# Moving the activation slots of a fused conv-attention block to one residue modulo 512

## The chip, the cores and the metric

The kernel runs on one core of one Trainium2 chip. The metric is the device time of one execution in microseconds; the kernel before took 2053.18 us (median of 3 runs, 2053.03 to 2053.26). The engines are named as in the profile: PE is TensorE (matmuls), PEld its weight loads, DVE is VectorE, ACT ScalarE, POOL GpSimd, SP the queue that issues the transfers.

## What is computed

One decoder block on x of 2,048 positions by 1,024 channels, float32. Two branches share one input projection of 7,680 columns and are merged by gates:

```
h    = rmsnorm(x) ; proj = h @ w_in            # 1024 x 7680
glu_in, conv_gate, q, k, v, attn_gate, merge = split(proj)
c    = silu(layernorm(depthwise_conv31(a * sigmoid(b))))
y_c  = (c * silu(conv_gate)) @ w_conv_out
att  = sliding-window attention (window 128, 16 heads, 4 kv heads, sinks)
y_a  = (att * silu(attn_gate)) @ w_attn_out
x    = x + (g_conv * y_c + g_attn * y_a) @ w_out ; out = rmsnorm(x)
```

## The kernel before

**Order of the work.** The sequence is taken in two sweeps of 1,024 positions. A sweep holds its normalised input transposed in 16 tiles `hT[half][k]`: half 0 or 1 for its 512 positions, k for the chunk of 128 input channels. It runs the 60 projections of 128 output columns, then 8 `ya` projections on the attention output `aT`, 8 `yc` projections on the gated convolution output `uT`, and last the output product `o`: 16 blocks of 24 matmuls, 384 in a sweep. The order on PE is written out by hand: the class `Line` keeps an estimated clock (`MM_US = 0.2275` for a matmul) and puts the steps of the attention, of the convolution and of the norms between the matmuls at due times. Attention is 32 units in a sweep, each with three visits to PE: scores `sc` (16 matmuls of 256 columns or fewer), transposes `tpp` (4 of 128 columns), and `ov` (4 matmuls of 512 columns, weights `vt` twice and `vd` twice).

**One projection.** Every product is made of three matmuls, since each operand is split into a high and a low part (`float32r`). In `project` (line 281) a half is 8 chunks by 3 matmuls, 24, each with its own weight load, all into one PSUM tile:

```
for half in halves:
    for k in range(KC):
        ... (whi, r[:, 0, :]), (whi, r[:, 1, :]), (wlo, r[:, 0, :])
            pe.matmul(out=ps, lhsT=a, rhs=b, ...)
```

The moving operand `r` is 512 columns of 4 bytes, 2,048 bytes of a partition: the high part begins at the start of a slot, the low part 2,048 bytes behind. The weights (`whi`, `wlo`) are 128 columns, 512 bytes, of a buffer of the pool `stage`, which starts where the slots end; chunk k lies at 512 times (k modulo 4) in it. In `o` (line 885) the moving operand is `wo` in a `c` slot and the weights are a 512-byte piece of `mT` in an `a` or `h` slot. In `ov` (line 622) the moving operands are `pt` and `pc`, the weights `vt` and `vd`, all in slots.

**Slots.** The pool `slots` has 43 buffers, named h0 to h15, a0 to a15, c0 to c7 and x0 to x2, each used by several tiles in turn. Normally a slot is 4,096 bytes of every partition. The 12 names in `WIDE` (all c, a14, a15, h14, h15) are 4,224 bytes, for a tile of 1,054 elements: the convolution's input `glu` with a halo of 30. `glu` only ever lies in c6, c7 and a14. The buffers lie behind one another in the order in which the program first asks for them; the first starts at byte 9,024 of the partition, which is 320 modulo 512 (and 832 modulo 2,048). Each wide slot pushes everything behind it by 128 bytes modulo 512. The starts modulo 512, in order:

| slots | before | after |
|---|---|---|
| a0-a5, h0-h7, a11, a12, a7-a10, c0 | 320 | 320 |
| c1 | 448 | 320 |
| c2 | 64 | 320 |
| c3 | 192 | 320 |
| c7 | 320 | 320 |
| h8-h14 | 448 | 320 |
| h15 | 64 | 320 |
| a6, a13, x0, x1, x2, a15 | 192 | 320 |
| c6 | 320 | 320 |
| a14 | 448 | 320 |
| c4 | 64 | 320 |
| c5 | 192 | 320 |
| raw, whi, wlo buffers | 320 | 320 |

**Which tile lies where.** In sweep 0 `hT` and later `uT` have half 0 in h0-h7 and half 1 in h8-h15; in sweep 1 half 0 in h8-h15 and half 1 in a0-a7. `aT` (and `mT`) lie in a0-a15 in sweep 0 and in h0-h7, a8-a15 in sweep 1. `vt` lies in a0-a3 (sweep 1: h0-h3), `vd` in x0-x2 and a15, `pt` and `pc` in a7-a10 (sweep 1: h7, a8-a10). Each `wo` chunk k lies in c0 to c7.

Of the kernel before, what the change touches and what calls it, by code (L numbers as in the profile page):

```python
# [19 lines left out]
P = 128  # L20
# [3 lines left out]
T = 1024  # L24
# [4 lines left out]
HALO = TAPS - 1  # L29
# [24 lines left out]
def hybrid_block(ctx: ExitStack, tc: tile.TileContext, x, par_d, w_in, w_conv, sinks, w_attn, w_out,  # L54
# [21 lines left out]
    A = [f"a{i}" for i in range(16)]  # L76
    C = [f"c{i}" for i in range(8)]
    X = [f"x{i}" for i in range(3)]
    WIDE = set(C) | {"a14", "a15", "h14", "h15"}

    def slot(tag, shape, dt, name):
        n = int(np.prod(shape[1:]))
        full = HALO + T + 2 if tag in WIDE else 1024
        t = slots.tile([P, full], dt, tag=tag, name=name)
        v = t[:, 0:n]
        if len(shape) == 3:
            v = v.rearrange("p (a b) -> p a b", b=shape[2])
        elif len(shape) == 4:
            v = v.rearrange("p (a b c) -> p a b c", b=shape[2], c=shape[3])
        return v  # L90
# [11 lines left out]
    def load_first(half):  # L102
        xs = []
        for j in range(4):
            r0 = (4 * half + j) * P
            xs.append(slot(A[7 * half + j], [P, D], F32, f"xf{half}_{j}"))
            nc.sync.dma_start(out=xs[-1], in_=x2[r0:r0 + P, :])
        return xs
# [4 lines left out]
    ident_r = const.tile([P, P], F32R, name="ident_r")  # L113
    ident = f(ident_r)
    ident_0 = slot(A[4], [P, P], F32, "ident_0")
    make_identity(nc, ident_0)
    dve.tensor_copy(out=ident_r, in_=ident_0)
    ones_0 = slot(A[5], [P, P], F32, "ones_0")
    dve.memset(ones_0, 1.0 / D)
    ones = const.tile([P, P], F32R, name="ones")  # L120
# [844 lines left out]
```

## Time and profile before

| | |
|---|---|
| median of 3 runs | 2053.18 us |
| the profiled execution's own time | 2053.2 us |
| its span, first to last instruction | 2051.5 us |
| granted TensorE clock, mean | 0.999 |
| matmuls | 9,256 |
| bytes moved | 355.91 MB, 173 GB/s mean |

The profiled execution stands 0.02 us from the median, and 1.7 us of its time lie around its span. Busy time of PE is modelled at the end of each matmul, so what is read below is the distance from the start of one matmul to the start of the next: the number of matmuls that begin in a stretch, against the length of the stretch. In a table of stretches the number in brackets behind x counts every matmul that is in work in the stretch, also one that began ahead of it.

### The profile page before, as it was taken

How to read it: one execution, taken by the hardware profiler on the slowest of the kernel's cores; microseconds unless marked ns; L12 is line 12 of the kernel's file. 1: busy time of each engine (PE TensorE's matmuls, PEld its weight loads, DVE VectorE, ACT ScalarE, POOL GpSimd, SP SyncE). 2: the span in 40 equal slices, each digit the busy share in tenths (PEclk: the TensorE clock that was granted, in tenths of full speed). 3: DMA queues.
4: the chain of work that ended last, by engine and by line, in shares of the span. 5: the costliest groups of instructions: out<-in, count | busy, mean ns of one | idle time of the engine just before them, and what ended most of it. 6: DMA issues, size and time to landing. Idle time of an engine off the chain costs nothing.

```text
span 2051.5 us, 27562 instructions
## 1 busy us (share of the span) xinstructions
PE 2031.3 (99%) x9256; PEld 1669.1 (81%) x9256; DVE 1327.4 (65%) x1965; ACT 1027.8 (50%) x2313; POOL 403.4 (20%) x336
## 2 busy tenths in 40 slices
PE   7999999999999999999999999999999999999998
PEld 6888888888888888888888888888888888888886
DVE  4968769988994355123668678689888924441323
ACT  6312477777777463123433125767677764621222
POOL 2335332333323223241001120111011100001200
PEclk9999999999999999999999999999999999999999
DMA  7445655555566757444344555555555577564422
GB/s 249 144 144 167 208 170 160 166 168 172 161 188 212 252 174 244 143 157 169 131 144 138 164 178 188 160 175 174 173 156 171 179 222 257 172 228 138 153 110 82
DMA packets 265821, 355.91 MB, mean 173 GB/s; under 512 B 28112, under 2 KB 126544, under 8 KB 265680
## 3 DMA queue, kind: packets, MB, share of 16 engines
q1 hardware_dynamic: 265680, 354.16, 53.3%
q8 instruction: 73, 1.20, 0.2%
q14 instruction: 68, 0.56, 0.1%
HBM read 234.51 MB, written 119.54 MB: 173 GB/s over the span
## 4 chain that ended last, share of the span: by engine, by line
PE 96%; DVE 2%; DMA 1%; issue 0%; SPq 0%; POOL 0%; ACT 0%; DVEq 0%; POOLq 0%
PE mm_cg L281 9%; PE o L885 9%; PE mm_ma L281 9%; PE mm_ga L281 9%; PE mm_mc L281 9%; PE mm_yc L281 9%; PE mm_ya L281 9%; PE mm_gb L281 8%; PE mm_ag L281 7%; PE mm_q_a L281 4%; PE mm_q_b L281 4%; PE sc L572 3%; PE ov L622 3%; PE mm_v L281 2%; DVE acc L396 2%; PE tpp L602 1%
## 5 line engine op out<-in xcount | busy, mean ns | idle before, releaser
L396 DVE SCALAR_TENSOR_TENSOR acc<-glu,par,acc 128x1024 f32<-128x1024 f32 x464 | 596.3, 1285 | 6.2
L885 PE MATMUL o<-wo,mT 128*128 128x512 f32 x768 | 181.3, 395 | 0.0
L885 PEld LDWEIGHTS o<-wo,mT 128*128 128x128 f32 x768 | 143.2, 188 | 32.0
L281 PE MATMUL mm_cg<-hT,whi_cg 128*128 128x512 f32 x512 | 161.1, 396 | 0.0
L281 PE MATMUL mm_ga<-hT,whi_ga 128*128 128x512 f32 x512 | 160.9, 395 | 0.2 <-ACT whi_ga L253 0.2
L281 PE MATMUL mm_ma<-hT,whi_ma 128*128 128x512 f32 x512 | 161.0, 396 | 0.0
L281 PE MATMUL mm_ag<-hT,whi_ag 128*128 128x512 f32 x512 | 160.8, 395 | 0.0
L281 PE MATMUL mm_gb<-hT,whi_gb 128*128 128x512 f32 x512 | 160.7, 395 | 0.0
L281 PE MATMUL mm_mc<-hT,whi_mc 128*128 128x512 f32 x512 | 159.7, 393 | 0.0
L281 PE MATMUL mm_yc<-uT,whi_yc 128*128 128x512 f32 x512 | 159.5, 393 | 0.0
L281 PE MATMUL mm_ya<-aT,whi_ya 128*128 128x512 f32 x512 | 158.7, 391 | 0.0
L613 POOL TENSOR_SCALAR_AFFINE_SELECT pc<-pt 128x1024 fp32r<-128x1024 f32 x60 | 65.6, 1094 | 428.7 <-DVE pt L242 428.6
L281 PEld LDWEIGHTS mm_yc<-uT,whi_yc 128*128 128x128 f32 x512 | 96.2, 188 | 21.8
L281 PEld LDWEIGHTS mm_mc<-hT,whi_mc 128*128 128x128 f32 x512 | 96.1, 188 | 21.7
L281 PEld LDWEIGHTS mm_ya<-aT,whi_ya 128*128 128x128 f32 x512 | 96.1, 188 | 20.9
L281 PEld LDWEIGHTS mm_ga<-hT,whi_ga 128*128 128x128 f32 x512 | 94.6, 188 | 20.4 <-ACT whi_ga L253 0.6
L281 PEld LDWEIGHTS mm_gb<-hT,whi_gb 128*128 128x128 f32 x512 | 94.7, 188 | 19.9
L281 PEld LDWEIGHTS mm_ag<-hT,whi_ag 128*128 128x128 f32 x512 | 94.3, 188 | 19.4
L281 PEld LDWEIGHTS mm_cg<-hT,whi_cg 128*128 128x128 f32 x512 | 94.2, 188 | 19.5
L281 PEld LDWEIGHTS mm_ma<-hT,whi_ma 128*128 128x128 f32 x512 | 94.2, 188 | 19.3
L592 ACT ACTIVATE ss<-ss,st 128x128 f32<-128x128 f32 x256 | 99.7, 391 | 11.2 <-DVE st L587 10.7
L281 PE MATMUL mm_ga<-hT,wlo_ga 128*128 128x512 f32 x256 | 100.8, 394 | 0.7 <-POOL wlo_ga L242 0.7
(364 smaller groups left out, 4259.3 us busy)
## 6 DMA issues: line engine op xcount, KB each, us to landing
qk<-d_q SPq DMA_DIRECT2D x256, 64.0 KB, 2.2
d_a<-ss SPq DMA_DIRECT2D x128, 128.0 KB, 1.9
aT<-d_a SPq DMA_DIRECT2D x32, 512.0 KB, 5.5
qk<-d_k SPq DMA_DIRECT2D x240, 64.0 KB, 2.0
raw_gb<-in_w_in_dram SPq DMA_DIRECT2D x34, 256.0 KB, 3.2
raw_ga<-in_w_in_dram SPq DMA_DIRECT2D x34, 256.0 KB, 3.3
raw_ag<-in_w_in_dram SPq DMA_DIRECT2D x32, 256.0 KB, 3.7
d_ag<-ag SPq DMA_DIRECT2D x32, 256.0 KB, 2.2
```

The source lines that it names most:

```text
L281: pe.matmul(out=ps, lhsT=a, rhs=b, start=(k == 0 and i == 0), stop=(k == KC - 1 and i == 2))
L396: dve.scalar_tensor_tensor(out=to, in0=glu[c][:, j:j + T], scalar=tap(c, j), in1=acc[c], op0=ALU.mult, op1=ALU.add)
L572: pe.matmul(out=o, lhsT=q[:, h, :], rhs=r, start=(j == 0), stop=(j == 1))
L592: act.activation(out=sb[:, h, :], in_=sb[:, h, :], func=AF.Exp, scale=SCALE, bias=ngm[:, h:h + 1], accum_out=den[:, h:h + 1])
L602: pe.transpose(out=tpp[:, h, :], in_=sb[:, h, :], identity=ident)
L613: pool.affine_select(out=pc, in_=f(pt), pattern=[[0, 2], [0, GQ], [1, P]], compare_op=ALU.is_ge, fill=0.0, base=0, channel_multiplier=-1)
L622: pe.matmul(out=ov, lhsT=vv, rhs=pp[:, i % 2], start=(i == 0), stop=(i == nm - 1))
L885: pe.matmul(out=ps, lhsT=a[:, c0:c0 + P], rhs=r, start=(k == 0 and i == 0), stop=(k == KC - 1 and i == 2))
```

## The change

The set of wide slots shrinks from twelve to the three that hold a `glu` tile, and those three grow from 4,224 to 4,608 bytes, which is 512 more than the others have. Three times 512 bytes are twelve times 128 bytes, so the pools behind the slots stay where they are. No instruction, wait, transfer or order changes; only the addresses of 22 slots do (the right column of the table above).

```
-    WIDE = set(C) | {"a14", "a15", "h14", "h15"}
+    WIDE = {"c6", "c7", "a14"}

     def slot(tag, shape, dt, name):
         n = int(np.prod(shape[1:]))
-        full = HALO + T + 2 if tag in WIDE else 1024
+        full = 1024 + P if tag in WIDE else 1024
```

## The prediction

> **What bounds the kernel now.** I read the page's busy shares and its clock line first, then the chain that ended last, then what PE waited for.
>
> ```profile
> span 2051.5 us, 27562 instructions
> PE 2031.3 (99%) x9256; PEld 1669.1 (81%) x9256; DVE 1327.4 (65%) x1965; ACT 1027.8 (50%) x2313; POOL 403.4 (20%) x336
> PEclk9999999999999999999999999999999999999999
> PE 96%; DVE 2%; DMA 1%; issue 0%; SPq 0%; POOL 0%; ACT 0%; DVEq 0%; POOLq 0%
> ```
> ```profile
> PE tpf L361 <- DVE ident_r L117: 8.4, 1, 8.4
> PE tpf L361 <- DVE xf L354: 2.4, 2, 1.5
> PE sc L572 <- DVE pt L242: 1.0, 1, 1.0
> PE mm_ga L281 <- POOL wlo_ga L242: 0.7, 1, 0.7
> PE tpf L361 <- DVE hT L364: 0.5, 1, 0.5
> PE mm_ga L281 <- ACT whi_ga L253: 0.2, 1, 0.2
> ```
>
> PE is the chain (96%). Its waits come to 13.2 us, 11.3 of them transposes of the opening (tpf); behind that it waits 1.9 us in two milliseconds. The clock is full in every slice. So the time is the number of matmuls times the distance between their starts, and the change can only act through that distance, or by making another engine late. The pieces of the chain give the distance:
>
> ```profile
> 147.28 11.04 PE mm_q_b L281 x48
> ...
> 764.63 87.99 PE mm_ya L281 x384
> 852.62 88.33 PE mm_yc L281 x384
> ...
> 1160.36 11.07 PE mm_q_b L281 x48
> ...
> 1779.53 87.67 PE mm_ya L281 x384
> 1867.19 88.57 PE mm_yc L281 x384
> 1955.77 88.72 PE o L885 x384
> ```
>
> These stretches hold matmuls of 512 columns with nothing between, at one clock, and yet run at 228.3 ns (87.67/384), 230.0, 230.7 and 231.0 ns. So I cut them into halves of 24 matmuls. In the table of stretches (length, PE busy, x in work, clock, transfers) one of the x is the matmul of the half before whose modelled end reaches in:
>
> ```profile
> 880.00:885.59 5.59, 5.59 (x25) 1.00 0.26 91
> 885.59:891.04 5.45, 5.45 (x25) 1.00 0.58 196
> 1900.24:1905.82 5.58, 5.58 (x25) 1.00 0.72 238
> 1905.82:1911.31 5.49, 5.49 (x25) 1.00 0.12 40
> 1375.84:1376.75 0.91, 0.91 (x5) 1.00 0.03 9
> 1376.75:1377.69 0.94, 0.94 (x5) 1.00 0.00 0
> 422.34:423.73 1.39, 1.39 (x8) 1.00 0.50 189
> 425.08:426.45 1.36, 1.36 (x7) 1.00 0.71 185
> 593.07:598.51 5.44, 5.44 (x25) 1.00 0.53 149
> ```
>
> Rows 1 and 2 are yc in sweep 0: half 1, with uT in h8-h15 (448, last chunk 64), takes 5.59 us, and half 0 in h0-h7 (320, as the weights) 5.45. Rows 3 and 4 are yc in sweep 1, where the places are swapped: now half 0 lies in h8-h15 and takes 5.58, half 1 in a0-a7, with only a6 off 320, 5.49. So it isn't the half, the sweep or the weights, which are the same, but the place of the moving tile. The two halves make the rows of 48 above: 5.59 + 5.45 is 11.04 and 5.58 + 5.49 is 11.07. Transfers don't explain it: the row with the busiest DMA (0.72) and the one with 0.26 are equally slow.
>
> Rows 5 and 6 turn the pair round: in one attention unit the four matmuls ahead of `ov` (moving and weights on 320) take 0.91, then `ov` itself 0.94, whose moving tiles lie on 320 while its last two weights, `vd`, lie on 192. So it is the pair of moving tile and weights that matters, not the moving tile alone. Rows 7 and 8 show six matmuls right behind a score visit, and six further on in the same half, all on 320: 1.39 and 1.36. A visit costs 0.03 until the rhythm is found again. Row 9 is a half on 320 within the attention stage: 5.44, 226.7 ns, the best there is.
>
> **The change part by part.** It adds and removes no instruction, wait or transfer; no queue is passed. What moves is the start of 22 slots, and every matmul of 512 columns gets the residue of row 2 for both operands. Gains, from the rows above, a half being 24 matmuls:
>
> 1. Sweep 0, half 1 (h8-h15): 60 projections and 8 yc, 68 halves × (5.59 − 5.45) = 9.5 us.
> 2. Sweep 1, half 0 (h8-h15): 68 × (5.58 − 5.45) = 8.8.
> 3. Sweep 1, half 1 (a6 off): 68 × (5.49 − 5.45) = 2.7.
> 4. ya: 384 matmuls at 5.45/24 = 227.1 ns would be 87.2 against 87.99 and 87.67: 1.3.
> 5. o: 88.72 − 87.2 = 1.5 in sweep 1, taken twice: 3.0. This is the least certain, see the rivals.
> 6. ov: 60 units with vd × 0.03 = 1.8, and the rhythm that needn't be found again behind it, another 0.03 each by rows 7 and 8: 1.8.
>
> Together 28.9. Off go the places where the rhythm is lost anyway: 64 score visits, 64 tpp and 32 other groups of transposes, 160 × 6 = 960 matmuls. Half of them lie in halves now off 320, and there six take 6 × 232.9 = 1.40, no more than the 1.39 with all on 320; the gain of 5.8 ns each, counted above, isn't there: 480 × 5.8 = 2.8 off. Half of term 5 goes off for its doubt, 1.5. That leaves 24.6; I take 24.
>
> The other engines. DVE, ACT and POOL instructions read and write slots that move. No row shows one of them by its slot, so this is bounded by size: the dearest is
>
> ```profile
> L396 DVE SCALAR_TENSOR_TENSOR acc<-glu,par,acc 128x1024 f32<-128x1024 f32 x464 | 596.3, 1285 | 6.2
> ...
> 226.00:420.00 194.00, 193.03 (x915) 160.00 (x915) 172.40 (x249) 138.53 (x337) 56.17 (x49) 1.00 0.54 172
> 420.00:560.00 140.00, 140.00 (x667) 115.97 (x666) 125.41 (x189) 100.06 (x247) 43.52 (x36) 1.00 0.53 168
> 1240.00:1480.00 240.00, 240.00 (x1139) 198.94 (x1138) 206.48 (x313) 168.90 (x415) 24.99 (x21) 1.00 0.56 172
> ```
>
> with 31 taps that start at 31 different offsets of 4 bytes and one mean of 1285 ns. One per cent more or less on its 596 us is 6 us on an engine that idles for 700: nothing, as long as DVE stays behind PE. Its fullest stage is 125.41 of 140 (90%); with PE 1.2% quicker that is 91%. So DVE, ACT and transfers are costed at nothing; the cover is this 9%, some 13 us of a stage of 140, and if it were gone PE's 1.0 us wait of sc on pt is the one that would grow. Behind the gain nothing else is late next: PE stays the chain. The transfers keep count, sizes and queue; each projection's weights are asked for one projection (11 us) ahead.
>
> One rule speaks against all of this. The Trainium skill, page "TensorE: Matmul & The Clock Gate", section "Step-by-step: what each phase is for", says that PE has two independent SBUF read ports, so that loading the next weights takes no read bandwidth from the running matmul. By it alone addresses shouldn't matter and the sum would be 0; rows 1 to 6 don't agree, unless something else than the address sets them apart.
>
> **The rivals.** *A, only the residue modulo more than 512 counts.* All moving tiles that are quick now start at 832 modulo 2,048. After the change h8-h15, a6, a13, x, a15 and c6 start at 1,344, a14 at 1,856, c4 and c5 at 320. If the moving tile needs 832, terms 1 to 4 fall away and only ov (3.6) and part of o stay: 2049. For it:
>
> ```profile
> 1959.76:1961.85 2.09, 2.09 (x10) 1.00 1.01 320
> ```
>
> nine matmuls of o in sweep 1 on c6, c7 and c0, all 320 modulo 512 with weights on 320, but 1,856, 1,344 and 832 modulo 2,048: 231.9 ns each, no rhythm found. Against it: within every half the weights step through all four multiples of 512 (chunk k at 512 times k modulo 4), and rows 2 and 9 stay at 5.45 and 5.44, so at least the weights' residue above 512 is free. And the nine of o come behind matmuls on slots off 320, so at least six of them are still finding the rhythm, as in row 7.
>
> *B, nothing happens.* Moving reads and weight loads don't touch each other, and something else than the residue slows h8-h15 (their place high in the partition, say, as all quick moving tiles lie low): 2053. The rule cited above would leave the time there. Against it ov, where weights low and high in the partition make the difference while the moving tile stays.
>
> *C, slower.* The new distance between h8-h15 and the weights locks into a worse rhythm than now, as the pair in ov does: 0.94/4 = 235.0 ns against 232.9 on terms 1 and 2, 136 halves × 24 × 2.1 ns = 6.9, so 2060. It decides from the point where a half on h8-h15 takes over 5.59. Only the ov row speaks for it, and that pair ends with this change.
>
> **How the numbers follow.** The profiled execution took 2053.2, 0.02 over the median: 2053.2 − 24 = 2029. Chances: forecast 0.83, A 0.07, B 0.06, C 0.04. Its own range: the low end is every half at 5.44 and no rhythm lost, 28.9 + 304 halves × 0.01 = 31.9, so 2021; the high end is that only the halves away from the attention gain, some 32 projections a sweep (18 ahead of it, 6 behind, 8 yc) × (0.14 + 0.13 + 0.04) = 9.9, and ya 1.3, so 2042. A lies beyond at 2049 and isn't needed for 8 in 10, so the range is 2021 to 2042. A measurement of this kernel can tell 0.2%, 4.1 us, from no change: faster is the forecast and a third of A, 0.85; same is B and the rest of A, 0.11; slower is C, 0.04.
>
> **What would show it.** Right: the chain's rows of 48 fall from 11.04 and 11.07 to 10.88 to 10.90 in both sweeps, yc and ya to 87.1 or 87.2, o to 87.2 to 88; halves 0 and 1 are alike; ov's four take 0.91; DVE's and ACT's means stay. Wrong: halves on h8-h15 stay at 5.58 (A or B; then ov tells them apart, 0.91 in A and 0.94 in B) or rise (C), or new waits of PE on DVE or ACT appear. Only o staying at 88.7 would mean that term 5 alone was wrong.

## The result, and the profile after

The changed kernel takes 2027.62 us (median of 4 runs, 2027.36 to 2027.86) against 2053.18: 25.56 us less, a ratio of 0.9876 with a 95% interval of 0.9858 to 0.9893. The forecast was 2029, range 2021 to 2042.

The page after, and PE's waits. The span is 25.6 us shorter, PE is still 99% busy, the clock is full, and the waits are the old ones: 13.8 us in place of 13.2.

```profile
span 2025.9 us, 27562 instructions
PE 2004.9 (99%) x9256; PEld 1666.9 (82%) x9256; DVE 1324.1 (65%) x1965; ACT 1026.0 (51%) x2313; POOL 403.4 (20%) x336
PEclk9999999999999999999999999999999999999999
...
L396 DVE SCALAR_TENSOR_TENSOR acc<-glu,par,acc 128x1024 f32<-128x1024 f32 x464 | 595.9, 1284 | 6.2
```
```profile
PE tpf L361 <- DVE ident_r L117: 8.4, 1, 8.4
PE tpf L361 <- DVE xf L354: 2.3, 2, 1.4
PE sc L572 <- DVE pt L242: 1.3, 1, 1.3
PE tpf L361 <- DVE hT L364: 0.9, 1, 0.9
```

The chain's pieces after. Every undisturbed row of 48 is 10.88 and every row of 384 is 87.04 or 87.05, 226.67 ns from start to start, in both sweeps and in all three products, which ran at 228.3 to 231.0 ns before. This steady distance is what is called the rhythm here and in the prediction:

```profile
145.72 10.88 PE mm_q_b L281 x48
...
756.66 87.04 PE mm_ya L281 x384
843.70 87.04 PE mm_yc L281 x384
...
1147.03 10.88 PE mm_q_b L281 x48
...
1757.77 87.04 PE mm_ya L281 x384
1844.81 87.04 PE mm_yc L281 x384
1931.85 87.05 PE o L885 x384
```

Halves of yc as in the prediction (half 0 and 1 in sweep 0, half 0 and 1 in sweep 1), then the ov of its row 6. All halves take 5.44, ov 0.91:

```profile
876.18:881.62 5.44, 5.44 (x25) 1.00 0.62 199
881.62:887.06 5.44, 5.44 (x25) 1.00 0.22 79
1877.29:1882.72 5.44, 5.44 (x25) 1.00 0.69 241
1882.72:1888.16 5.44, 5.44 (x25) 1.00 0.14 49
1360.45:1361.36 0.91, 0.91 (x5) 1.00 0.00 0
```

Transfers at a share of 0.14 and of 0.69 leave a half at 5.44 alike.

Where the 25.6 us came from, by the sum of the distances between starts of matmuls in the two traces (first to last matmul: 2035.71 us before, 2010.12 after):

```
                                   before   after    less   term of the prediction
projections, yc  sweep 0 half 1    381.29   372.75   8.53   1:  9.5
                 sweep 1 half 0    381.03   372.85   8.18   2:  8.8
                 sweep 1 half 1    375.63   372.59   3.04   3:  2.7
                 sweep 0 half 0    376.27   375.24   1.03   none
ya                                 175.65   174.08   1.57   4:  1.3
o                                  178.44   175.54   2.90   5:  3.0, half taken off
ov                                  57.80    56.21   1.59   6:  3.6 with what follows it
score visits                        61.58    62.81  -1.22   none
transposes, layernorm                                -0.03
sum                                                 25.6    24.6, taken as 24
```

### The profile page after: what moved, and what is told of

It is laid out like the page before. It is cut to its first block, busy times and chain, and to the rows that moved or that the text cites. A ratio compares the mean times of both kernels' runs of the same rounds, so it can differ in the third digit from the quotient of the medians.

```text
span 2025.9 us, 27562 instructions
## 1 busy us (share of the span) xinstructions
PE 2004.9 (99%) x9256; PEld 1666.9 (82%) x9256; DVE 1324.1 (65%) x1965; ACT 1026.0 (51%) x2313; POOL 403.4 (20%) x336
## 4 chain that ended last, share of the span: by engine, by line
PE 94%; DVE 4%; DMA 1%; issue 0%; ACT 0%; SPq 0%; POOL 0%; DVEq 0%; ACTq 0%; POOLq 0%
PE mm_ma L281 9%; PE o L885 9%; PE mm_mc L281 9%; PE mm_yc L281 9%; PE mm_ya L281 9%; PE mm_ga L281 9%; PE mm_gb L281 8%; PE mm_cg L281 8%; PE mm_ag L281 6%; PE mm_q_a L281 4%; PE mm_q_b L281 4%; PE sc L572 3%; DVE acc L396 3%; PE ov L622 2%; PE mm_v L281 2%; PE tpp L602 1%
## 5 line engine op out<-in xcount | busy, mean ns | idle before, releaser
L396 DVE SCALAR_TENSOR_TENSOR acc<-glu,par,acc 128x1024 f32<-128x1024 f32 x464 | 595.9, 1284 | 6.2
L281 PEld LDWEIGHTS mm_ag<-hT,whi_ag 128*128 128x128 f32 x512 | 94.2, 188 | 18.3
```

Of the source, the lines that this page charges most:

```text
L281: pe.matmul(out=ps, lhsT=a, rhs=b, start=(k == 0 and i == 0), stop=(k == KC - 1 and i == 2))
L396: dve.scalar_tensor_tensor(out=to, in0=glu[c][:, j:j + T], scalar=tap(c, j), in1=acc[c], op0=ALU.mult, op1=ALU.add)
```

## The experiments

Left open by the result: whether the start of the moving tile or its distance from the weights counts, modulo what, which of the weight loads it is that counts, and whether another distance is better still. Names: theory P is the distance, R the start itself. In all of these kernels instructions and order are those of the changed kernel; unused buffers are laid between the others to move them.

**Everything moved by 128 bytes.**

```
     dve.memset(v_last, 0.0)
+    const.tile([P, 32], F32, name="pad")
```

> The changed kernel with 128 bytes more ahead of the slots, so that every slot and every weight buffer starts at 448 modulo 512, the residue on which h8-h15 were slow before. Theory P (the distance between the moving tile and the weights modulo 512 counts; it is still 0): 2027.6 us, at most 1 us off, halves of 24 matmuls at 5.44 us. Theory R (the start of the moving tile itself counts, and 320 is a good one, 448 a bad one): every half at 5.58 to 5.59, 304 halves x 0.145 = 44 us more, and o 768 x 6 ns = 5 us more, about 2076 us.

2027.93 us, ratio to the kernel before 0.9878 (0.9862 to 0.9895); two halves of yc in sweep 0:

```profile
875.40:880.85 5.44, 5.44 (x25) 1.00 0.62 201
880.85:886.28 5.44, 5.44 (x25) 1.00 0.25 74
```

On 448, the residue that h8-h15 had when they were slow, everything is as quick as on 320. R falls.

**Only the weights moved by 128 bytes.**

```
+    stage.tile([P, 32], F32, tag="pad", name="pad", bufs=1)
     x2, out2 = x[0], out[0]
```

> The changed kernel with 128 bytes more between the slots and the weight buffers: all slots stay at 320, raw, whi and wlo go to 448. Theory P: all 304 halves of the projections, ya and yc go from 5.44 to about 5.58, 44 us more, about 2071 us, slower than the kernel before, while o (weights and moving tile both in slots) stays at 87.05 us for 384 matmuls and ov's four matmuls at 0.91 us. Theory R: no change, 2027.6 us.

2064.79 us, slower than before the change: 1.0057 (1.0042 to 1.0072). Halves 0 and 1 of yc in sweep 0, and the chain's pieces of sweep 1:

```profile
892.38:897.95 5.57, 5.57 (x25) 1.00 0.60 192
897.95:903.53 5.58, 5.58 (x25) 1.00 0.25 82
```
```profile
1790.46 89.23 PE mm_ya L282 x384
1879.69 89.22 PE mm_yc L282 x384
1968.91 87.05 PE o L886 x384
```

No moving tile was touched and all projections are slow; o, whose two operands lie in slots, is not. That is P. The size was missed by 6 us. Away from the attention the matmuls of the projections lose 5.9 ns each, as the 44 us have it; the 3,483 between the first and the last attention unit of a sweep lose 4.5, which makes 5.4 us less. Near the attention's visits the rhythm is lost anyway, as in the main result.

**Only h8-h15 put back to 448.** Pads of 128 bytes ahead of h8 and 384 behind h15.

> The changed kernel with only h8 to h15 put back to 448 modulo 512, all else at 320. If terms 1 and 2 of the prediction are sized right (136 halves on h8-h15, 0.13 to 0.14 us each, 18.3 us), and the halves behind them lose their first few matmuls again (0.01 to 0.03 each), then 2046 to 2050 us; yc 11.03 to 11.04 us per projection in both sweeps. Were h8-h15 not the place of the gain, it would stay below 2035 us. Theories P and R say the same here.

2047.59 us, 0.9973 (0.9963 to 0.9984). yc, halves 0 and 1 of sweep 0, then of sweep 1:

```profile
884.93:890.38 5.46, 5.46 (x25) 1.00 0.58 194
890.38:895.97 5.59, 5.59 (x25) 1.00 0.27 79
1896.41:1902.00 5.59, 5.59 (x25) 1.00 0.77 235
1902.00:1907.45 5.46, 5.46 (x25) 1.00 0.16 41
```

The slow halves go with h8-h15 from half 1 to half 0. The eight slots are worth 20.0 of the 25.6 us. The well-placed halves take 5.46 instead of 5.44: their first three matmuls, behind a slow half, take 231, 232 and 230 ns from start to start, the others 227.

**Other distances, three and three and two in one kernel.** Pads of other sizes at the same places; for 16 bytes the view of h0-h7 starts 4 elements into the slot.

> Three distances in one kernel: h0-h7 start 64 bytes above the weights' residue, h8-h15 192, a0-a15 and c0-c3 256. Read from the quiet yc: sweep 0 half 0 is 64, half 1 192; sweep 1 half 0 192, half 1 256. Theory P with a period of 512: all three slow, 5.50 to 5.62 us for 24 matmuls, the whole 2055 to 2080 us. Theory P with a shorter period: 256 (period 256) or 64, 192 and 256 (period 64) as quick as 5.44.

> As the last one with 96 on h0-h7, 448 on h8-h15 and 32 on a0-a15. Theory P with a period of 512 and a sharp optimum at 0: all slow, 5.50 to 5.62. If what counts is the same 64-byte piece, 32 is as quick as 5.44 and 96 and 448 are slow. A distance quicker than 0, under 5.43, is not expected by either.

> As the last two with 320 on h0-h7, 224 on h8-h15 and 128 on a0-a15. Theory P with a period of 512: all slow, 5.50 to 5.62; 128 repeats what h8-h14 were before (5.58 to 5.59). None quicker than 5.44.

> The changed kernel with h0-h7 16 bytes above the weights' residue and h8-h15 160; a0-a15 and c0-c7 at 0 modulo 256. Read in the quiet yc: sweep 0 half 0 is 16, half 1 is 160. If a distance under a 64-byte or 32-byte piece were free, 16 would take 5.44; since 32 took 5.59 to 5.60, it is expected slow, 5.50 to 5.61, and 160 too, 5.55 to 5.61. Neither is expected under 5.44.

They took 2053.76, 2070.29, 2062.88 and 2057.02 us, one run each; the first is under the 2055 to 2080 expected, since 256 was not slow. First kernel: yc on 64, 192 and 192, then a half 0 of ya in sweep 0 on 256 (half 1 takes the same):

```profile
887.43:892.93 5.50, 5.50 (x25) 1.00 0.59 195
892.93:898.52 5.59, 5.59 (x25) 1.00 0.27 83
1901.19:1906.80 5.60, 5.60 (x25) 1.00 0.70 239
799.76:805.20 5.44, 5.44 (x25) 1.00 0.82 260
```

Second: yc on 96, 448 and 32. Third: yc on 320, 224, 224 and 128. Fourth: yc on 16 and 160.

```profile
894.85:900.46 5.61, 5.61 (x25) 1.00 0.55 189
900.46:906.06 5.59, 5.59 (x25) 1.00 0.25 82
1922.73:1928.33 5.59, 5.59 (x25) 1.00 0.15 44
```
```profile
889.98:895.47 5.49, 5.49 (x25) 1.00 0.58 194
895.47:901.08 5.61, 5.61 (x25) 1.00 0.26 84
1910.50:1916.10 5.60, 5.60 (x25) 1.00 0.69 231
1916.10:1921.70 5.60, 5.60 (x25) 1.00 0.14 43
```
```profile
891.20:896.75 5.56, 5.56 (x25) 1.00 0.57 191
896.75:902.37 5.62, 5.62 (x25) 1.00 0.27 81
```

256 is as good as 0. 320 and 64 give the same 5.49 to 5.50, and 448 and 192 the same 5.59. So the distance counts modulo 256, not 512. Modulo 256: 0 takes 5.44; 64 takes 5.49 to 5.50; 16 takes 5.56; the others in these rows (32, 96, 128, 160, 192, 224) 5.59 to 5.62. None is under 5.44.

These kernels hold one distance more, in o of sweep 1, where blocks 0 to 3 take their weights from h0-h7 and the moving tile from the `c` slots. In the fourth kernel the weights there lie 16 bytes above the moving tile, so the distance is -16, which is 240 modulo 256. Block 1:

```profile
1966.52:1971.96 5.44, 5.44 (x25) 1.00 0.59 220
```

240 is as good as 0, while 16 takes 5.56 in yc, so it matters which of the two lies higher. That rests on one kernel, and 16 itself wasn't tried in o; where o and yc have the same distance they agree: 64 takes 5.49 in o of the third kernel, 192 takes 5.60 in o of the first and the second.

**256 bytes instead of 512.**

```
-        full = 1024 + P if tag in WIDE else 1024
+        full = 1024 + P // 2 if tag in WIDE else 1024
```

> The changed kernel with the three glu slots 256 bytes longer than the others in place of 512, so that the slots lie at 64 or 320 modulo 512, all at 64 modulo 256. In the run with distances 64, 192 and 256, ya with a distance of 256 took 5.44 us a half, as at 0. Theory P256 (the distance modulo 256 counts): 2027.6 us, at most 1 us off, h8-h15 at 5.44. Theory P512 (modulo 512, and the quiet ya was quick for another reason): h8-h15 slow again, 136 halves x 0.14 and their neighbours, 2046 to 2050 us as with h8-h15 put back.

2027.72 us, 0.9879 (0.9864 to 0.9894), with h8-h15 on 64 modulo 512 and the rest partly on 320:

```profile
876.59:882.03 5.44, 5.44 (x25) 1.00 0.62 202
882.03:887.47 5.44, 5.44 (x25) 1.00 0.26 77
```

The period of 256 shows in the time of a whole kernel as well, and three slots 256 bytes longer do what the change does with 512.

**Hopping pairs in o.** Pads ahead of h2, h4, h6, a11, c2 and c6, and other lengths of c6, c7 and a14, so that h2, h3, h6, h7, c2, c3, c6 and c7 lie 128 higher and the rest where it was.

> The changed kernel with h2, h3, h6, h7, c2, c3, c6 and c7 at 448 modulo 512, everything else at 320. In o of sweep 1 the blocks 0 to 3 take weights from h0-h7 and the moving tile from c0-c7, so each matmul's own two operands stay at the same residue, but both hop by 128 every two chunks; blocks 4 to 7 take weights from a8-a15 (320), so chunks 2, 3, 6 and 7 have a distance of 128. Theory P: blocks 0 to 3 take 5.44 to 5.48 us for 24 matmuls, blocks 4 to 7 5.50 to 5.56. Theory S (what counts is that the moving tiles follow one another on one residue, or that each lies on 320): both kinds of block equally slow, 5.50 to 5.56. Theory N (the pair is the moving tile and the next matmul's weights, whose load runs beside it): blocks 0 to 3 between, since 4 of 24 pairs are off and the rhythm is lost four times, 5.48 to 5.53. The time of the whole is over the changed kernel's, 2032 to 2045 us, as h2, h3, h6 and h7 are off the weights in the projections.

2036.24 us, one run. o of sweep 1, a block with weights from h0-h7 (both operands hop together), then one with weights from a8-a15:

```profile
1944.72:1950.20 5.48, 5.48 (x25) 1.00 0.62 226
1966.68:1972.22 5.53, 5.53 (x25) 1.00 0.00 0
```

5.48 stands on the border of P and N, so the single distances decide. Mean ns from start to start by position in the two middle blocks of each four, chunks 0 to 5 of 8:

```
together  230 226 227 | 226 226 233 | 230 226 227 | 226 226 233 | 230 226 227 | 226 226 233 | ...
apart     232 233 230 | 227 227 226 | 234 224 237 | 229 238 229 | 232 232 231 | 227 226 227 | ...
```

S falls: the hop costs little when the weights hop too. But what it costs falls on the matmul ahead of the hop: its own operands match, and it takes 233 since the weights loaded beside it, the next matmul's, are 128 away. In the second row the matmul ahead of the hop, whose next weights stay, takes 226. So a matmul is slowed by the next one's weights, as N has it.

**Only wlo moved by 128.** One pad ahead of the wlo buffers.

> The changed kernel with the wlo buffers alone 128 bytes further, so that of the three matmuls of a chunk the third has its own weights off the moving tile, while the second has the next matmul's weights off it. Theory N (the moving tile against the next matmul's weights, loaded beside it): from start to start 226-227, 232-234, about 230 ns in the steady order whi, whi, wlo; the slow one is the second, so that the wlo group's mean duration isn't above the whi group's. Theory P in the narrow sense (the matmul's own two operands): the third is the slow one, 230, 226, 233, and wlo's mean lies above whi's. Both: 24 matmuls about 5.50 us, the whole 2043 to 2052 us.

2055.73 us, one run; over the 2043 to 2052 expected. A half of yc, and its two groups:

```profile
888.73:894.28 5.55, 5.55 (x25) 1.00 0.59 193
```
```profile
L284 PE MATMUL mm_yc<-uT,whi_yc 128*128 128x512 f32 x512 | 159.4, 393 | 0.0
...
L284 PE MATMUL mm_yc<-uT,wlo_yc 128*128 128x512 f32 x256 | 101.6, 397 | 0.0
```

From start to start it is 227, 233, 234 in every chunk. The second is slow, whose own weights match and whose next don't: N. The third, whose own don't match and whose next do, is slow as well: by N alone it had to be 230, and the wlo group's mean would not lie above whi's (397 against 393).

The weight loads in the traces narrow this down. In yc of the changed kernel the load of the next matmul's weights starts 3 ns behind the start of a matmul and lasts 188 ns; a matmul's own load has ended some 35 ns before it starts. So what is read beside the moving tile is the next one's weights. Here and in the hop kernel alike, the load beside the matmul that follows a slow one lasts 192 ns, and all others last 188. That points to the third carrying the after-effect of the second, as the 230 behind the hop's 233 does. Why it takes 234 and not 230 isn't explained: a cost of its own is not ruled out.

**The transposes' identity on the same residue.**

```
+    const.tile([P, 48], F32, name="pad_a")
     ident_r = const.tile([P, P], F32R, name="ident_r")
...
     dve.memset(v_last, 0.0)
+    const.tile([P, 16], F32, name="pad_b")
```

> The changed kernel with 192 bytes ahead of the identity matrix (moving tile of the transposes) and 64 behind the constants, so that the identity lies on the slots' residue modulo 256 too (it was 64 above it); slots and weights keep theirs. 96 groups of 4 transposes. If the distance costs the transposes or the matmuls behind them something, up to 6 matmuls of 0.03 us in all per group and a few ns per transpose, it is up to 4 us quicker, 2024 us. If the transposes are bound otherwise, 2027.6 us, at most 1 us off; this is the likelier, since before the change transposes with ss on 320 and on 192 took the same 88.6 ns.

2027.87 us, 0.988 (0.9863 to 0.9896), and the transposes are as they were with the identity off (272 ns after the change, here 271). Between a distance of 64 and one of 0 their price doesn't change, and before the change the `ss` tiles on 192 cost the same 88.6 ns from start to start as those on 320. Other distances weren't tried.

```profile
L604 PE MATMUL tpp<-ident_r,ss 128*128 128x128 f32 x256 | 38.2, 271 | 0.0
```

No kernel tried here beats the changed one.

## Why the prediction was right

*What bounds the kernel* held: PE's chain, matmuls times distance. The reading of rows 1 to 4, that it is the place of the moving tile, and of rows 5 and 6, that it is the pair with the weights, is what the first three experiments show. The rule of the Trainium skill that was set against it (page "TensorE: Matmul & The Clock Gate", section "Step-by-step: what each phase is for": two independent read ports, a weight load takes nothing from the running matmul) doesn't hold here to the last 3%: with the weights alone moved by 128 bytes a half goes from 5.44 to 5.57 or 5.58. Another rule of the Trainium skill agrees: "DMA never contends with a compute engine" (page "SBUF — State Buffer", section "Who interferes with whom"), by the shares of 0.14 and 0.69 with one and the same 5.44.

*The terms.* Terms 1 and 2 came out at 16.7 for 18.3: 1.6 short, less than the 2.8 taken off for the places where the rhythm is lost anyway. Terms 3 and 4 were a little small, since settled halves are 5.44 and not the 5.45 that I counted with. Term 5 was right as first worked out, 2.9 for 3.0 (1.23 in sweep 0, 1.67 in sweep 1), and wrongly halved: the nine matmuls on c6, c7 and c0 made me doubt it, and after the change o runs at 87.05 like the rest. Why those nine found no rhythm before isn't explained. Their starts modulo 2,048 are not the cause: after the change o reads c6 and c7 at 1,344 and c0 at 832, and ya of sweep 1 reads a14 at 1,856, all at 5.44. Term 6 gave 1.6 for 1.8 in ov itself; its other 1.8, behind ov, lies in the rows of the projections and isn't told apart there. Left out were 1.0 gained in sweep 0's half 0, which no longer follows a slow half, and 1.2 lost in the score visits. That only 1.4 us stand between 2029 and 2027.6 is in part luck: these errors, and the 0.6 by which 24.6 was rounded down, cancel.

*The other engines* were costed at nothing, and that held but for the score visits. DVE's conv operation takes 1284 for 1285. But a score visit (8 matmuls, 512 in all in the 64 visits, not 16 as said above) writes into two PSUM tiles, and its fifth matmul, the first into the second tile, can wait for DVE. The two distances around it are 120 ns normally. Before, they were longer in one visit, by 1.2 us; after, in five, by 2.3 us together. In each of the five the weight load of the fifth matmul starts some 54 ns after a `pt` instruction of DVE ends, which reads a PSUM tile of the same pool. One of the new ones:

```profile
403.12 0.68 DVE L242 TENSOR_TENSOR pt<-tpp,pt 128x512 fp32r<-128x512 f32 x1
403.86 0.30 PEld L572 LDWEIGHTS sc<-qk 128*128 128x128 f32 x2 [0.29 <-DVE pt L242]
```

So PE, now quicker, has to wait for DVE's `pt` more often. It is the wait that the prediction named as the one that would grow; it priced it at nothing, and it took back 1.1 us. The list of waits, from 1.0 to 1.3, shows only the longest of them.

*The rivals.* A (more than modulo 512) falls: h8-h15 lie at 1,344 modulo 2,048 and run at 5.44. The period is less than 512, not more. B falls, as h8-h15 haven't left their place high in the partition. C falls with the same halves. What I took over unasked was the 512: the rows of before had h15, c2 and c4 on 64, which is 320 modulo 256, but only in runs of three matmuls: c2 and c4 between slow ones, h15 behind 21 slow ones (229, 237 and 228 ns in yc of sweep 0), too short to show it.

## What to carry to other kernels

Where TensorE is the chain and loads new weights for each matmul, compare the distance between starts of the same matmul on different buffers: one form, one clock and two rates is a sign of their places. Here 24 matmuls of 512 columns, with moving tiles and weights of 4-byte elements that start on one residue modulo 256 bytes, took 5.44 us where most other distances took 5.57 to 5.62, for some pad bytes and no instruction. Other element sizes and shapes weren't tried. Pad such buffers by whole 256 bytes, and don't let a buffer whose length is no multiple of 256 stand in front of others. And see what the quicker engine meets: here it waited for DVE in five places instead of one.

## What was not expected of the hardware

- How far the moving tile starts above the weights matters modulo 256 bytes. Of the distances tried only 0 and 240 (5.44 us for 24 matmuls) and, less so, 64 (5.49) are good; 32 bytes already cost 5.59, 16 bytes 5.56. Why just these is open.
- At distance 0 the rhythm is exact: 226.67 ns in every undisturbed stretch, 87.04 or 87.05 us for 384, with all buffers on 320, all on 448 or (the kernel with 256) on 64 and 320 mixed, by the program's layout.
- It goes by the next matmul's weights at least, whose load runs beside the matmul (it starts 3 ns behind it): in o with hopping pairs the matmul ahead of the hop takes 233 ns and the others 226 to 230.
- Behind an interruption some matmuls pass until the 226.67 are found again: three behind a slow half in the kernel with h8-h15 put back (231, 232, 230 ns; 5.46 against 5.44 us a half), five behind a score visit in the changed kernel (237, 235, 229, 232 and 230 ns on the mean).
